# Expert matrices loaded with two neighbouring rows per partition, and features kept in pairs

## The chip, the cores and the metric

The kernel runs on one core of a Trainium2 chip. The metric is the device time of one execution in microseconds (us), lower is better. All times below come from runs of the kernel before the change and from one profiled execution of it.

## The reference

Two layers of a transformer over 256 latent tokens and 256 context tokens of 1,024 features each. A layer has two parts. The first modulates its input, projects it once, and feeds four mixers (three attentions and a 2-D Fourier transform), gates and merges them and projects the result. The second is the one that the change touches, a mixture of 16 experts in which each expert chooses 32 tokens of a stream:

```python
def expert_choice_ffn(h, w_router, w_gate, w_up, w_down):
    cap = max(1, EC_CAPACITY * n // N_EXPERTS)            # 32
    aff = softmax(einsum("bnd,de->bne", h, w_router))
    sel_w, sel_idx = lax.top_k(swapaxes(aff, 1, 2), cap)
    xs = vmap(lambda hb, ib: hb[ib])(h, sel_idx)
    a = einsum("becd,edf->becf", xs, w_gate)
    u = einsum("becd,edf->becf", xs, w_up)
    y = einsum("becf,efd->becd", silu(a) * u, w_down) * sel_w[..., None]
    # rows of y are added back at their tokens
```

Both parts end in a residual and a layer norm. In layer 0 both streams go through the mixture (64 rows an expert), in layer 1 the latents alone (32 rows). All data are float32. An expert has three matrices of 1,024 x 1,024, 4 MB each, so the two mixtures read 2 x 16 x 12 MB.

## The kernel before, in words

**Loads.** Weights stream from HBM in tiles of 1 MB, nearly all issued by SyncE (SP) in one fixed order. `ex_raw` (L359) describes a quarter of an expert matrix, 256 rows: `(k p) n -> p k n` with p = 128, so partition p receives row p and row 128 + p, two runs of 4 KB that lie 512 KB apart in HBM and side by side in SBUF. Where the tile is one piece (`raw`, `w8`, `q8`, `k8`, `cst`, `wbr`) one DMA brings it (L376). Where it is a list (`p`, `pt`, `b4`: two tiles of 512 KB; `wbs`: four of 256 KB) each piece has a DMA of its own (L374). The last expert's `w_down` comes by columns instead, a quarter of the columns of all rows at a time, in runs of 1 KB (L365). The planner at the end of the program (L1682 to L1720) keeps the loads up to 16 tiles ahead of their use, in the order in which the units of work use them; a tile's load waits until the work that last used its buffer is done. `ring` says which buffers the experts take in turn: in layer 1 a cycle of 18 holds one `p` and one `pt`, in layer 0 no list.

**An expert.** `gu0` and `gu1` multiply the gathered token rows by gate and up, taking the quarters in the order in which they are loaded (gate 0, up 0, gate 1, and so on); `swiglu` is on ScalarE (ACT, L1077) and VectorE (DVE, L1078, L1079); `down0` and `down1` transpose the result in four blocks of 128 features on TensorE (PE: L1102 in layer 0, L1129 in layer 1), copy it out of PSUM on ACT, and multiply by `w_down` (L1109, L1136). Tokens are gathered by one-hot products (`gather`, L996, transposes at L1012; `gather_one`, L1023, transposes at L1038), and a group of four experts is scattered back by `scat` (L1146). The last group and the last expert have their own steps (`scat_hl` L1152, `scat_start` L1195, `last_hT`, `last_down` L1216, `last_scat`).

**Feature order.** Contraction block kt holds the features kt x 128 to kt x 128 + 127 everywhere. Transposes take contiguous blocks of 128 columns: `turned` (L904) for the router, the gathers and the downs. `mod_tr` (L243, products at L250) and `load_b`, `load_ln` (L171, L178) bring modulation vectors, biases and norm gains into the same order, `small_loads` (L453) the router's weights, and `g_bcast` (L315) spreads a gate vector over all partitions and copies it out of PSUM on ACT (L324).

**Order of work.** SP and GpSimd (POOL) issue in the program's order. PE, ACT and DVE are ordered by the framework's scheduler, except where `inorder` fixes it. In layer 0, `load_b` and `load_ln` for layer 1 run within the gates (L1383).

Of the kernel before, what the change touches and what calls it, by code (L numbers as in the profile page):

```python
# [16 lines left out]
D = 1024  # L17
# [69 lines left out]
def trunk(ctx: ExitStack, tc: tile.TileContext, x, c, ctx_in, c_ctx, w_mod, b_mod, w_in, qk_gain,  # L87
# [52 lines left out]
    def load_consts(l):  # L140
        """The mixers' tables, which give their place to weights once a layer's attention is done."""
        mix_cst.append(big([128, N_MIX], "cst"))
        nc.sync.dma_start(mix_cst[-1], consts[:, 0:N_MIX])
        if l == 0:
            nc.sync.dma_start(route_cst, consts[:, N_MIX:N_CONST])
# [10 lines left out]
    def ones():  # L156
        # the last column of the triangle
        return const("tri")[:, 127:128].to_broadcast([128, 128])
# [12 lines left out]
    def load_b(l):  # L171
        bsrc = t2([48, 128])
        G.dma_start(bsrc, b_mod[l].rearrange("(k p) -> k p", p=128))
        p = ps_t([128, 48])
        T.transpose(p, bsrc, ident[0:48, 0:48])
        V.tensor_copy(bT[l], p)

    def load_ln(l):  # L178
        lsrc = t2([32, 128])
        for n, v in enumerate((ln1_g, ln1_b, ln2_g, ln2_b)):  # L180
            G.dma_start(lsrc[8 * n:8 * n + 8], v[l].rearrange("(k p) -> k p", p=128))
        p = ps_t([128, 32])
        T.transpose(p, lsrc, ident[0:32, 0:32])
        V.tensor_copy(lnT[l].rearrange("p n k -> p (n k)"), p)
# [25 lines left out]
    def mod_mm(l, ch, group):  # L210
        """Partial products of one chunk, in rows 2q and 2q + 1 of each quadrant (q the chunk's place in its four)."""
# [14 lines left out]
    def mod_acc(l, ch, group):  # L226
        """As mod_mm, but the chunks of a group add up in a bank of their own."""
# [15 lines left out]
    def mod_tr(l, group):  # L243
        """Sums of up to four chunks, feature-major."""
# [4 lines left out]
        for g in range(4):  # L249
            T.matmul(p[:, g], mrows[l, group][:, g * 128:g * 128 + 128], sel[:, 0:8], start=True, stop=True)  # L250
# [8 lines left out]
    def mod_first(kp):  # L259
        """Shift and scale of two feature tiles, the first layer's."""  # L260
# [32 lines left out]
    def affine(l, half):  # L293
        """u = z * A + B, feature-major: the modulation, with the norm's own gain and bias folded in."""
# [20 lines left out]
    def g_bcast(l, m, j, ns=range(2)):  # L315
        t = gbc[l, m, j] if (l, m, j) in gbc else b4([128, D])
        gbc[l, m, j] = t
        for n in ns:
# [5 lines left out]
            A.activation(t[:, n * 512:n * 512 + 512], p, AF.Copy)  # L324

# [33 lines left out]
    def ex_raw(l, e, kind, q):  # L359
        w = {"g": w_gate, "u": w_up, "d": w_down}[kind]  # L360

        if e == NE - 1 and kind == "d":
            # the last expert's share of the output comes by columns
# [4 lines left out]
        rows = w[l, e, q * 256:q * 256 + 256, :].rearrange("(k p) n -> p k n", p=128)  # L368

        def go(t):  # L370
# [4 lines left out]
            else:  # L375
                nc.sync.dma_start(t, rows)  # L376
        return (("ex", l, e, kind, q), [128, 2, D], go)

    def ex_w(l, e, kind, k, c, n):
        """Rows k * 128.. and columns c..c + n of an expert's matrix."""  # L380
# [24 lines left out]
    def inorder(*engines):  # L405
        """What the block puts on these engines issues after the previous such block's work."""
# [10 lines left out]
    def split(key, src, alloc, eng=V):  # L417
        """hi + lo parts, each exact in the product's 12-bit significand."""
# [25 lines left out]
    def small_loads(l):  # L444
# [8 lines left out]
        G.dma_start(wr[:, 0:8], w_router[l].rearrange("(k p) e -> p k e", p=128))  # L453
        st_["small"] = {"gq": gq, "snk": snk, "wr": wr}

    def layer(l):
# [7 lines left out]
        def ut_alloc():  # L464
            if last:
                # a tile per stream: the context's go after the projections
# [33 lines left out]
        def bias_table():  # L500
            """Per-row relative-position bias, 8x, flipped into token order."""
# [47 lines left out]
        def rope(src, t, nh):  # L549
            """Rotates src [128, nh, 64] in place."""  # L550
# [11 lines left out]
        def post_norm(m, t):  # L562
            """Values aside; the norm's factors."""
# [15 lines left out]
        def post_vec(m, t):  # L579
            """norm and rotation of one token tile, split."""  # L580
# [26 lines left out]
        def post_tr(m, t):  # L607
            """q blocks [hi | lo] ([lo | hi] for the second kv head), k blocks [hi | hi] x 2, [lo0 | lo1]."""
# [19 lines left out]
        def br_out(m, src, kv, ts):  # L628
            """src [128, kv, tokens] to the branch, split."""
# [195 lines left out]
        def residual(dst, z, key):  # L825
            """alpha times the norm's output, from its normalised rows."""
# [6 lines left out]
        def y0_mm(kt):  # L833
            """Left half of the output: one merged feature tile's share, all tokens."""
# [45 lines left out]
        NS = NT // 2  # L880

        def route_weights():
            """The norm and the modulation folded into the router: logits = rstd * (h.wA - mean * sum(wA)) + B.w"""
# [15 lines left out]
        def turned(t, hf):  # L899
            """Half of the features of a token tile, feature-major."""  # L900
            pt = ps_t([128, 4, 128])
            u = t2([128, 4, 128])
            for k in range(4):
                T.transpose(pt[:, k], st_["h"][t][:, (4 * hf + k) * 128:(4 * hf + k) * 128 + 128], ident)  # L904
# [3 lines left out]
        def route_half(t, hf):  # L908
            """Router products of one half of the features of a token tile."""
# [4 lines left out]
            for k in range(4):  # L914
                # rows 0..15 of a quadrant sum its share; rows 16..31 are not used
# [20 lines left out]
        def route(t):  # L936
            """Router probabilities of one token tile; its rows normalised."""
# [14 lines left out]
        def rows(t):  # L952
            """Normalises a token tile."""
# [795 lines left out]
```

## Time and profile before

| | us |
|---|---|
| median of three runs | 1805.77 |
| lowest and highest | 1802.51, 1806.38 |
| span of the profiled execution, first to last instruction | 1799.7 |

The profiled execution is known by its span; what lies around the span is seen only as the difference to the median, 6.1 us. The two mixtures lie at about 540 to 1010 us (layer 0) and 1320 to 1790 us (layer 1) of that span. The page divides the span into 40 slices of 45 us; DMA there is the mean busy share of the core's 16 DMA engines. A busy PE in such a slice may still be a PE that waits often and briefly, because the ends of pipelined matmuls are modelled. The idle time before an instruction, and what ended it, is in the views by waits and in order of time.

### The profile page before, as it was taken

To read this page: it belongs to the slowest core of one execution; us is meant where nothing else is said; L and a number is where in the kernel's file an instruction comes from. 1 tells how busy PE (TensorE), PEld (TensorE's weight loads), DVE (VectorE), ACT (ScalarE), POOL (GpSimd) and SP (SyncE) were. 2 spreads that over 40 slices of the span, in tenths; PEclk is the share of its full clock that TensorE was granted. 3 is DMA by queue.
4 is the path that set the end of the run, shared out by engine and by line. 5 is a ranking of instruction groups with operands and counts; after the bars stand their busy time and mean duration, and the time that the engine had idled before them with its cause. 6 is when DMAs were issued, how large, how long until landed. Compare 5 with 4: busy or idle time off the path is not lost.

```text
span 1799.7 us, 22915 instructions
## 1 busy us (share of the span) xinstructions
PE 1575.4 (88%) x9291; PEld 892.1 (50%) x9291; DVE 694.8 (39%) x1378; ACT 432.3 (24%) x929; POOL 129.7 (7%) x176
## 2 busy tenths in 40 slices
PE   7999999999989989899998899999978666667666
PEld 4767777768864333323332578888832211112112
DVE  3454453554452332222222585747543111102114
ACT  2343433343231110201200354544321001001000
POOL 1200112111110000000000320111100000000000
PEclk9999999999989999999999999999989889888888
DMA  9444344444559999999999664646889999999996
GB/s 310 164 149 157 119 167 107 164 140 165 216 208 365 374 408 409 409 409 409 409 409 403 234 240 169 216 111 236 327 317 409 409 409 409 409 409 409 409 409 245
DMA packets 194120, 533.04 MB, mean 296 GB/s; under 512 B 9520, under 2 KB 61088, under 8 KB 194016
## 3 DMA queue, kind: packets, MB, share of 16 engines
q1 hardware_dynamic: 192016, 527.49, 76.9%
q0 software_dynamic: 1856, 4.02, 1.3%
q8 instruction: 73, 1.20, 0.3%
q14 instruction: 31, 0.25, 0.0%
q10 hardware_dynamic: 144, 0.07, 0.0%
HBM read 530.50 MB, written 1.05 MB: 295 GB/s over the span
## 4 chain that ended last, share of the span: by engine, by line
PE 67%; DMA 15%; issue 10%; DVE 5%; ACT 2%; POOL 1%; SPq 0%; ACTq 0%; DVEq 0%; POOLq 0%
PE mm L771 14%; PE mm L1088 12%; PE mm L531 7%; DMA w<-in_w_up_dram 6%; PE mm L1109 5%; DMA raw<-in_w_up_dram 4%; PE mm L782 3%; PE pt L217 2%; PE mm L1122 2%; PE mm L851 2%; PE ps L1005 2%; DMA w<-in_w_down_dram 2%; PE ps L643 2%; PE pt L724 1%; PE ps L642 1%
## 5 line engine op out<-in xcount | busy, mean ns | idle before, releaser
L771 PE MATMUL mm<-w,b 128*128 128x512 f32 (+1 forms) x1536 | 292.6, 342 | 0.3 <-DVE b L424 0.3
L771 PEld LDWEIGHTS mm<-w,b 128*128 128x128 f32 x1536 | 236.8, 189 | 47.7 <-issue 18.6
L1077 ACT ACTIVATE t<-mm 128x512 f32<-128x512 f32 (+1 forms) x32 | 19.0, 594 | 663.2 <-PE mm L1122 352.1
L1078 DVE SCALAR_TENSOR_TENSOR t<-t,mm 128x512 f32<-128x512 f32 (+1 forms) x32 | 21.9, 684 | 358.6 <-ACT t L1077 358.5
L424 DVE TENSOR_TENSOR b<-raw,b 128x1024 fp32r<-128x1024 f32 (+1 forms) x95 | 112.7, 1189 | 122.7 <-ACT b L422 119.7
L531 PE MATMUL mm<-b,w 128*128 128x512 f32 (+1 forms) x720 | 148.9, 360 | 5.2 <-ACT b L422 3.6
L531 PEld LDWEIGHTS mm<-b,w 128*128 128x128 f32 x720 | 115.9, 192 | 30.7 <-ACT b L422 4.0
L422 ACT ACTIVATE b<-raw 128x1024 fp32r<-128x1024 f32 (+1 forms) x96 | 97.9, 1021 | 128.9 <-PE mm L771 97.5
L1095 DVE TENSOR_TENSOR k<-mm,b 32x512 f32<-32x512 f32 (+1 forms) x96 | 53.1, 553 | 187.5 <-PE mm L1109 84.6
L1088 PE MATMUL mm<-w,b 128*64 128x512 f32 x480 | 116.9, 596 | 2.1 <-DMA w<-in_w_gate_dram 1.2
L1122 PE MATMUL mm<-w,b 128*32 128x512 f32 x416 | 82.5, 665 | 26.9 <-DMA w<-in_w_up_dram 22.3
L800 POOL TENSOR_TENSOR b<-b,t 128x256 f32<-128x256 f32 x72 | 56.4, 798 | 521.6 <-DVE t L794 502.4
L1122 PE MATMUL mm<-raw,b 128*32 128x512 f32 x256 | 55.4, 733 | 30.8 <-DMA raw<-in_w_up_dram 16.1
L782 PE MATMUL mm<-w,wbs 128*128 128x512 f32 (+1 forms) x384 | 78.4, 339 | 0.1
L1088 PEld LDWEIGHTS mm<-w,b 128*64 128x64 f32 x480 | 37.9, 137 | 70.3 <-issue 63.9
L1088 PE MATMUL mm<-raw,b 128*64 128x512 f32 x280 | 70.9, 594 | 0.7 <-DMA raw<-in_w_gate_dram 0.7
L782 PEld LDWEIGHTS mm<-w,wbs 128*128 128x128 f32 x384 | 61.2, 188 | 8.8 <-ACT w L631 0.3
L1109 PE MATMUL mm<-w,t 128*64 128x512 f32 x240 | 58.4, 612 | 2.9 <-ACT t L1104 2.9
L1122 PEld LDWEIGHTS mm<-w,b 128*32 128x32 f32 x416 | 16.3, 116 | 86.8 <-DMA w<-in_w_up_dram 41.4
L681 ACT ACTIVATE p<-ps,st 128x512 f32<-128x512 f32 (+1 forms) x72 | 43.6, 613 | 55.3 <-DVE st L679 55.3
L1146 PE MATMUL ps<-k,wbs 128*128 128x512 f32 x72 | 39.7, 671 | 4.7 <-DVE k L1095 3.7
L1122 PEld LDWEIGHTS mm<-raw,b 128*32 128x32 f32 x256 | 9.8, 118 | 65.8 <-DMA raw<-in_w_up_dram 28.7
(373 smaller groups left out, 2232.6 us busy)
## 6 DMA issues: line engine op xcount, KB each, us to landing
w<-in_w_up_dram SPq DMA_DIRECT2D x64, 1024.0 KB, 18.1
w<-in_w_down_dram SPq DMA_DIRECT2D x59, 1024.0 KB, 16.6
raw<-in_w_mod_dram SPq DMA_DIRECT2D x48, 1024.0 KB, 5.2
w<-in_w_gate_dram SPq DMA_DIRECT2D x48, 1024.0 KB, 18.3
raw<-in_w_in_dram SPq DMA_DIRECT2D x46, 1024.0 KB, 6.3
raw<-in_w_down_dram SPq DMA_DIRECT2D x35, 1024.0 KB, 16.1
raw<-in_w_up_dram SPq DMA_DIRECT2D x34, 1024.0 KB, 15.3
raw<-in_w_gate_dram SPq DMA_DIRECT2D x33, 1024.0 KB, 15.3
```

Source lines behind the costliest of these rows:

```text
L422: A.activation(hi, src, AF.Copy)
L424: eng.tensor_tensor(lo, src, hi.bitcast(F32), op=OP.subtract)
L531: T.matmul(p, uu(kt, t * 128, t * 128 + 128), ww[:, kt % 2, a:n], start=kt == 0 and i == 0, stop=kt == 7 and i == 2)
L681: A.activation(P[:, hh, a:b], s[:, hh, a:b], AF.Exp, scale=0.125, bias=nm[:, n:n + 1], accum_out=rs[:, n:n + 1])
L771: T.matmul(p, ww[:, kt], uu(kt, 0, NTOK), start=n == 0, stop=n == 23)
L782: T.matmul(p, ww[:, k, o:o + 128], br[i][:, j, k], start=n == 0, stop=n == 5)
L800: G.tensor_tensor(m, m, e[:, c], op=OP.add)
L1088: T.matmul(p[fh * 64:fh * 64 + 64], xs[kt // 4][:, kt % 4, e % 4], ex_w(l, e, kind, kt, fh * 512, 512), start=kt == 0, stop=kt == 7)
L1095: V.tensor_tensor(dst, pd[q], g, op=OP.mult)
L1109: T.matmul(pd[dh * 64:dh * 64 + 64], hT[:, q, fh * 64:fh * 64 + 64], ex_w(l, e, "d", f, dh * 512, 512), start=f == 0, stop=f == 7)
L1122: T.matmul(p[r:r + 32], xs[kt // 4][:, kt % 4, e % 4], ex_w(l, e, kind, kt, fh * 512, 512), start=kt == 0, stop=kt == 7)
L1146: T.matmul(p[:, dh], loc["sm", gr][:, s, t], loc["y", gr][s][:, dh * 512:dh * 512 + 512], start=True, stop=True)
```

## The change

A quarter of an expert matrix is now loaded as `(p k) n -> p k n`: partition p receives rows 2p and 2p + 1, which are neighbours in HBM, as one run of 8 KB. Block kt of a contraction therefore holds every second feature of a stretch of 256: `paired(kt)` gives the columns 256 (kt // 2) + kt % 2, in steps of 2. All that meets these blocks is put in the same order: the transposes of `turned`, `gather`, `gather_one`, `down0` and `down1` read with a step of two elements; so do the products in `mod_tr` for all chunks but the first four; `load_b` and `load_ln` transpose both the plain and the paired order; the router's weights are loaded in pairs; `g_bcast` puts the plain order back with a copy that writes with a step of two. The matmuls with expert weights read the same places of the tiles as before. Loads into lists keep their pieces of 4 KB a partition, and the last expert's `w_down` keeps its columns and the plain order. Comments were taken out as well, which is left out here.

```diff
     def load_b(l):
-        bsrc = t2([48, 128])
-        G.dma_start(bsrc, b_mod[l].rearrange("(k p) -> k p", p=128))
-        p = ps_t([128, 48])
-        T.transpose(p, bsrc, ident[0:48, 0:48])
-        V.tensor_copy(bT[l], p)
+        bsrc = t2([24, 256])
+        G.dma_start(bsrc, b_mod[l].rearrange("(k p) -> k p", p=256))
+        p = turned_both(bsrc, 24)
+        b = bT[l].rearrange("p (q k) -> p k q", k=2)
+        V.tensor_copy(b[:, :, 0:8], p[:, 0, :, 0:8])
+        V.tensor_copy(b[:, :, 8:24], p[:, 1, :, 8:24])
 
     def load_ln(l):
-        lsrc = t2([32, 128])
+        lsrc = t2([16, 256])
         for n, v in enumerate((ln1_g, ln1_b, ln2_g, ln2_b)):
-            G.dma_start(lsrc[8 * n:8 * n + 8], v[l].rearrange("(k p) -> k p", p=128))
-        p = ps_t([128, 32])
-        T.transpose(p, lsrc, ident[0:32, 0:32])
-        V.tensor_copy(lnT[l].rearrange("p n k -> p (n k)"), p)
+            G.dma_start(lsrc[4 * n:4 * n + 4], v[l].rearrange("(k p) -> k p", p=256))
+        p = turned_both(lsrc, 16)
+        b = lnT[l].rearrange("p n (q k) -> p k (n q)", k=2)
+        V.tensor_copy(b[:, :, 0:8], p[:, 1, :, 0:8])
+        V.tensor_copy(b[:, :, 8:16], p[:, 0, :, 8:16])
...
+    def paired(kt):
+        c = kt // 2 * 256 + kt % 2
+        return slice(c, c + 255, 2)
+
+    def turned_both(src, n):
+        p = ps_t([128, 2, 2, n])
+        for k in range(2):
+            T.transpose(p[:, 0, k], src[:, k * 128:k * 128 + 128], ident[0:n, 0:n])
+            T.transpose(p[:, 1, k], src[:, k:k + 255:2], ident[0:n, 0:n])
+        return p
@@ mod_tr
         for g in range(4):
-            T.matmul(p[:, g], mrows[l, group][:, g * 128:g * 128 + 128], sel[:, 0:8], start=True, stop=True)
+            c = paired(g) if group[0] > 3 else slice(g * 128, g * 128 + 128)
+            T.matmul(p[:, g], mrows[l, group][:, c], sel[:, 0:8], start=True, stop=True)
@@ g_bcast
-            A.activation(t[:, n * 512:n * 512 + 512], p, AF.Copy)
+            A.activation(t[:, n * 512:n * 512 + 512].rearrange("p (q i k) -> p q k i", q=2, k=2),
+                         p.rearrange("p (q k i) -> p q k i", q=2, k=2), AF.Copy)
@@ ex_raw
-        rows = w[l, e, q * 256:q * 256 + 256, :].rearrange("(k p) n -> p k n", p=128)
+        rows = w[l, e, q * 256:q * 256 + 256, :].rearrange("(p k) n -> p k n", p=128)
...
-                nc.sync.dma_start(t, rows)
+                nc.sync.dma_start(t.rearrange("p k n -> p (k n)"), rows.rearrange("p k n -> p (k n)"))
@@ small_loads
-        G.dma_start(wr[:, 0:8], w_router[l].rearrange("(k p) e -> p k e", p=128))
+        G.dma_start(wr[:, 0:8].rearrange("p (q k) e -> p q (k e)", k=2),
+                    w_router[l].rearrange("(q p k) e -> p q (k e)", p=128, k=2))
@@ turned
-                T.transpose(pt[:, k], st_["h"][t][:, (4 * hf + k) * 128:(4 * hf + k) * 128 + 128], ident)
+                T.transpose(pt[:, k], st_["h"][t][:, paired(4 * hf + k)], ident)
@@ gather
-                T.transpose(p[:, q].rearrange("p n e c -> p (n e c)"), rows[:, q * 128:q * 128 + 128], ident)
+                T.transpose(p[:, q].rearrange("p n e c -> p (n e c)"), rows[:, paired(q)], ident)
@@ gather_one
-                T.transpose(p[:, k].rearrange("p q c -> p (q c)"), rows[:, k * 128:k * 128 + 128], ident)
+                T.transpose(p[:, k].rearrange("p q c -> p (q c)"), rows[:, paired(k)], ident)
@@ down0
-                T.transpose(p[:, q], a[:, q * 128:q * 128 + 128], ident)
+                T.transpose(p[:, q], a[:, paired(q)], ident)
@@ down1
-                T.transpose(p[:, q], a[:, q * 128:q * 128 + 128], ident[0:64, 0:64])
+                T.transpose(p[:, q], a[:, paired(q)], ident[0:64, 0:64])
```

## Rows read from the trace of the kernel before

**Rows 1.** The page of the profiled execution, part 2: the span in 40 slices of 45 us, busy tenths of PE and of the 16 DMA engines, and GB/s.

```profile
...
PE   7999999999989989899998899999978666667666
...
DMA  9444344444559999999999664646889999999996
GB/s 310 164 149 157 119 167 107 164 140 165 216 208 365 374 408 409 409 409 409 409 409 403 234 240 169 216 111 236 327 317 409 409 409 409 409 409 409 409 409 245
...
```

**Rows 2.** Busy time by stretch, from one call that cuts the span into eight: stretch, its length, busy us of each engine with its instructions, granted TensorE clock, busy share of the 16 DMA engines, GB/s.

```profile
...
540.00:650.00 110.00, 101.28 (x496) 43.11 (x494) 35.10 (x73) 19.09 (x54) 1.47 (x4) 1.00 0.96 377
650.00:945.00 295.00, 276.58 (x1258) 97.34 (x1256) 75.84 (x131) 30.83 (x67) 1.47 (x4) 0.99 1.03 409
945.00:970.00 25.00, 19.45 (x85) 5.20 (x81) 2.04 (x3) 1.20 (x2) 0.00 (x0) 1.00 1.03 409
970.00:1010.00 40.00, 38.52 (x186) 17.29 (x187) 16.30 (x29) 7.30 (x14) 3.07 (x5) 1.00 0.96 344
...
1340.00:1768.00 428.00, 297.79 (x2150) 91.13 (x2150) 76.02 (x154) 30.92 (x78) 3.57 (x6) 0.87 1.03 409
...
```

**Rows 3.** DMA packets of the stretch 700 to 900 us, in layer 0's mixture, where the data packets are 4 KB (the 1,245 small ones are completion marks): count, bytes, rate.

```profile
...
DMA packets 21195, 81.81 MB, mean 409 GB/s; under 512 B 1245, under 2 KB 1245, under 8 KB 21186
...
```

**Rows 4.** The same for 989 to 993 us, the last expert's column loads, whose runs are 1 KB.

```profile
...
DMA packets 1381, 1.39 MB, mean 348 GB/s; under 512 B 21, under 2 KB 1381, under 8 KB 1381
...
```

**Rows 5.** The same for 1031.3 to 1032.486 us, the second load of the constants (L143), whose runs are 7,936 bytes.

```profile
...
DMA packets 64, 0.51 MB, mean 428 GB/s; under 512 B 0, under 2 KB 0, under 8 KB 64
...
```

**Rows 6.** PE's weight loads in order of time, 940 to 972 us: start, busy us, line, operation, tiles, count, and in brackets the idle time before the first of them and what ended it.

```profile
...
943.87 0.14 PEld L1088 LDWEIGHTS mm<-w,b 128*64 128x64 f32 x2 [0.28 <-issue]
...
946.87 0.20 PEld L1088 LDWEIGHTS mm<-w,b 128*64 128x64 f32 x4 [1.13 <-DMA w<-in_w_up_dram]
...
949.42 0.20 PEld L1088 LDWEIGHTS mm<-w,b 128*64 128x64 f32 x4 [1.50 <-DMA w<-in_w_gate_dram]
...
951.99 0.20 PEld L1088 LDWEIGHTS mm<-w,b 128*64 128x64 f32 x4 [1.51 <-DMA w<-in_w_up_dram]
...
954.55 0.20 PEld L1088 LDWEIGHTS mm<-w,b 128*64 128x64 f32 x4 [1.50 <-DMA w<-in_w_gate_dram]
...
957.11 0.20 PEld L1088 LDWEIGHTS mm<-cst,b 128*64 128x64 f32 x4 [1.50 <-DMA cst<-in_w_up_dram]
...
964.79 0.20 PEld L1109 LDWEIGHTS mm<-wbr,t 128*64 128x64 f32 x4 [0.83 <-DMA wbr<-in_w_down_dram]
...
967.35 0.20 PEld L1109 LDWEIGHTS mm<-raw,t 128*64 128x64 f32 x4 [1.50 <-DMA raw<-in_w_down_dram]
...
969.96 0.19 PEld L1088 LDWEIGHTS mm<-raw,b 128*64 128x64 f32 x2 [1.56 <-PE mm L1109]
...
```

**Rows 7.** The chain that ended last within 940 to 1010 us, in order of time: start, us, what.

```profile
...
951.25 18.61 DMA raw<-in_w_gate_dram
...
969.99 1.04 PE mm L1088 x2
...
996.08 0.70 DVE t L1079
...
```

**Rows 8.** Expert loads by rows (L376) that were issued from 640 to 660 us: time from issue to landing.

```profile
...
DMA to landing us min/median/max: 6.9/9.6/11.3
```

**Rows 9.** The same, issued from 740 to 760 us.

```profile
...
DMA to landing us min/median/max: 18.1/18.5/18.8
```

**Rows 10.** DMA issues by tile and source: count, KB each, median us from issue to landing.

```profile
...
p<-in_w_gate_dram SPq DMA_DIRECT2D x16, 512.0 KB, 16.5
pt<-in_w_up_dram SPq DMA_DIRECT2D x16, 512.0 KB, 15.3
...
p<-in_w_down_dram SPq DMA_DIRECT2D x8, 512.0 KB, 15.9
pt<-in_w_down_dram SPq DMA_DIRECT2D x8, 512.0 KB, 15.5
...
```

**Rows 11.** What PE waited for from 1340 to 1760 us, longest in total first: us in total, times, longest.

```profile
...
PE mm L1122 <- DMA w<-in_w_up_dram: 22.3, 18, 1.5
PE mm L1122 <- DMA raw<-in_w_up_dram: 16.1, 12, 1.6
...
```

**Rows 12.** PE's matmuls in order of time at the end of layer 1 (columns as in rows 6).

```profile
...
1783.97 1.07 PE L1223 MATMUL mm<-w,t 128*32 128x256 f32 x16 [1.17 <-DMA w<-in_w_down_dram]
...
```

**Rows 13.** Weight loads of PE by line and shape: line, engine, operation, tiles, shape, count | busy us, mean ns of one | idle us before them.

```profile
...
L1012 PEld LDWEIGHTS pt<-idsel,t 128*128 128x128 f32 x84 | 8.8, 142 | 39.8 <-DVE t L1008 33.8 <-ACT t L1009 4.1 <-issue 1.6
...
L1102 PEld LDWEIGHTS pt<-idsel,t 128*128 128x128 f32 x60 | 7.2, 146 | 12.4 <-DVE t L1079 10.3 <-ACT wbs L1070 1.8 <-issue 0.2
...
L250 PEld LDWEIGHTS pt<-idsel,t 128*128 128x128 f32 x48 | 5.8, 191 | 0.8 <-issue 0.3 <-ACT b L422 0.2
...
L904 PEld LDWEIGHTS pt<-idsel,pt 128*128 128x128 f32 x16 | 2.0, 159 | 1.6 <-PE pt L928 1.1 <-issue 0.4
...
```

**Rows 14.** PE in order of time, 76 to 88 us, around the transpose in `load_ln` (columns as in rows 6).

```profile
...
82.97 0.24 PE L183 MATMUL pt<-idsel,t 32*128 32x32 f32 x1
83.14 5.11 PE L771 MATMUL mm<-w,b 128*128 128x512 f32 x21
```

**Rows 15.** PE in order of time, the first 8 us (columns as in rows 6).

```profile
...
7.42 1.08 PE L274 MATMUL ps<-raw,c_st 128*32 128x256 f32 x8 [0.89 <-DMA raw<-in_w_mod_dram]
```

**Rows 16.** ACT by line and shape (columns as in rows 13): the copy in `g_bcast`.

```profile
...
L324 ACT ACTIVATE b<-mm 128x512 f32<-128x512 f32 x12 | 7.2, 599 | 7.9 <-PE mm L321 7.9
...
```

## The prediction

> **What bounds the kernel now.** I read the page's slices first: PE is near full nearly everywhere, and the DMA engines are full in two stretches, at 409 GB/s, slices 15 to 22 and 31 to 39 [rows 1]. These are the two mixtures. Where two resources look full, the one that ends last must be found stretch by stretch, so I cut the span at the places where the picture changes [rows 2].
>
> In layer 1 from 1340 to 1768 us the DMA share is 1.03 throughout and PE is busy for 298 of 428 us: the loads bind. The waits say the same, with PE's longest ones on tiles of `w_up` that were still landing [rows 11], and a wait for `w_down` as late as 1784 us [rows 12].
>
> Layer 0 is less plain. From 650 to 945 us DMA is full, but PE is busy for 277 of 295 us. Here PE sets the pace and the loads run ahead. Only from 945 to 970 us does PE fall to 19.5 of 25. The reader is to see in PE's weight loads how the usual idle time of 0.28 us between pairs becomes 0.8 to 1.6 us at the head of each tile: eight such waits, 11.03 us together, less eight times 0.28 us is 8.8 us lost to late tiles; the one named after PE is a wait for a tile of `w_gate` in the chain [rows 6, 7]. From 970 us on the chain is PE alone until 996 us, and PE is busy for 38.5 of the 40 us to 1010 us [rows 2, 7]. So layer 0 can give no more than about 9 us to a faster load.
>
> **What a longer run is worth.** The rate depends on the length of the run. At 4 KB the trace shows 409 GB/s, which is 16 x 4,096 B / 409 = 160.2 ns a packet on each of 16 engines; at 1 KB 348 GB/s, or 47.1 ns; at 7,936 B 64 packets in 1.186 us, four on each engine, or 296.5 ns, 428 GB/s [rows 3, 4, 5]. The third row also shows that a run above 4 KB isn't cut up. A run of 8,192 B isn't in the trace. The line through the rows of 1 and 4 KB gives 311 ns, the one through 4 KB and 7,936 B gives 305.6 ns. Two packets of 4 KB cost 320.4 ns. A tile is eight runs of 8 KB on each engine, so it gains 0.075 to 0.118 us of its 2.563 us (1,048,576 B at 409 GB/s). I take 0.11 us, near the upper end, because 7,936 B is nearly the length in question; the rest is left for the completion marks, which that row hardly holds.
>
> The Trainium skill speaks against that ("DMA: Bandwidth & Descriptors", Specifications): it puts line rate at runs of 512 B and more, by which the change would bring nothing; the trace disagrees, with 348, 409 and 428 GB/s [rows 3 to 5]. The same page of the Trainium skill (Why small descriptors are slow) gives a fixed cost of about 3 cycles a packet, which at its 850 MHz is an estimate of 0.028 us a tile, and by it the sum below would be about 1800 us.
>
> **Layer 1.** 428 us at 2.563 us is 167 tiles. One is left out for a norm's gain and bias (two loads of 512 KB on SP, by the code). Lists keep their runs of 4 KB: the issues of `p` and `pt`, 24 each at half a tile [rows 10], are 24 tiles, of which the code's ring puts two ahead of 1340 us, so 22. That leaves 144 tiles x 0.11 = **15.8 us** (10.8 to 17.0). PE doesn't stand in the way, with 30% of the stretch idle; the last loads, by columns, keep their 1 KB, and what follows them is only shifted. DMA stays last.
>
> **Layer 0.** A faster queue gains only while it is never empty. Loads issued from 640 to 660 us land after 9.6 us, those from 740 to 760 us after 18.5 us [rows 8, 9]: around 650 us the queue is short, because tiles wait for buffers that PE still reads, and then it grows. I count the gain from there: to 957 us, 307 / 2.563 = 120 tiles x 0.11 = 13.2 us (9.0 to 14.2). This is more than the 8.8 us that PE lost, so I take **8.8 us**. Next late is PE itself, in its unbroken run after 970 us. The four microseconds left over end as tiles that lie ready earlier.
>
> **What is added.** `load_b` and `load_ln` run twice each and have three more transposes a time, 12 in all. In `load_ln` one holds PE for 0.17 us, from 82.97 to the next product at 83.14 us [rows 14]. Three run in the first 8 us, where PE waits 0.9 us for weights anyhow [rows 15]; nine x 0.17 = **1.5 us** on the path. Their second copy on DVE, four in all, is hidden by DVE's slack beside PE in the gates; uncovered it would be under 1 us.
>
> Transposes and products with a step of two read their stationary operand with that step: 60 loads at L1102, 56 of the 84 at L1012 in layer 0, 48 at L904 and 12 at L1038 (the code's counts), 176 at about 0.14 us; and 40 of the 48 at L250 at 0.19 us [rows 13]. Layer 1's at L1012 and L1129 lie under the wait for tiles. No row shows a stepped weight load. From below: nothing, as no engine reads fewer elements. From above: twice as long, 176 x 0.14 + 40 x 0.19 = 32.2 us, all on PE's path. I take nothing, as the number of elements, rows and instructions is the same. In the Trainium skill ("SBUF — State Buffer", Door 1) two reads in a 16-byte line suffice for full rate, which a step of two float32 gives; no run here shows it.
>
> `g_bcast` writes with a step on ACT, 12 copies at 0.6 us [rows 16]: between nothing and another 7.2 us if each took twice as long and none were hidden; I take nothing, since the element count stays. No DMA is added and none changes its place on SP or POOL; those of biases, gains and router weights have fewer, longer runs. The planner's order stays, and no wait is added.
>
> **Sum.** -15.8 - 8.8 + 1.5 = -23.1 us on a span of 1799.7 us, so 1776.6 us. The median run is 6.1 us above the span; the forecast is 1805.8 - 23.1 = 1782.7 us, **1783 us**. A change under 0.2%, 3.6 us, could not be told from none.
>
> **Rivals.**
> 1. Layer 0 gives nothing: tiles stay as late as the buffers that PE frees, or PE's order comes out worse. For it speaks that PE has only 18 of 295 us free there [rows 2]; against it the queue that grows to 18.5 us [rows 9]. 1805.8 - 15.8 + 1.5 = 1791.5 us.
> 2. The rate stays at 409 GB/s, because full-size tiles from many rows are limited by something else than the price of a packet, or because the run is cut in two. For it: the row of 7,936 B is a stretch of 1.2 us only. Against it: that row, and the line of the other two. Only the added 1.5 us are left, 1807.3 us. This is also what the line rate that the Trainium skill states would come to.
> 3. Slower: stepped weight loads. If each took twice as long, PE would pay 32.2 us in the router, the modulation and layer 0's mixture, where PE is the pace already, and the gain would be outrun: 1782.7 + 32.2 = 1814.9 us. It decides from a price of about 72% more a load (23.1 / 32.2). Nothing in the profile speaks for it, and nothing excludes it.
>
> **How the numbers follow.** Forecast 0.66, rival 1 0.15, rival 2 0.11, rival 3 0.08. The forecast's own spread, from 0.118 us a tile with the transposes hidden (-17.0 - 8.8 = -25.8) to 0.075 us (-10.8 - 8.8 + 1.5 = -18.1), is 1780 to 1788 us; one run differs from another by some 4 us. The range from 1777 to 1800 us holds it and rival 1, about 0.8. Faster 0.81, same 0.11 (rival 2), slower 0.08 (rival 3).
>
> **What would show it.** Right: packets of 8 KB in the mixtures and a rate near 428 GB/s from 650 to 960 and in layer 1; PE's waits at the head of tiles gone between 945 and 970 us; each of layer 1's experts about 1.2 us shorter. Weight loads at L1102 and L1012 still near 0.14 us. Wrong: a rate of 409 or less; stepped loads of 0.24 us and more; an order of PE's work in which a down waits for something that it did not wait for before.

## The result

| | median us | lowest, highest | kernel before beside it | ratio, 95% interval |
|---|---|---|---|---|
| changed kernel | 1794.53 | 1793.57, 1796.26 | 1805.42 | 0.9944 [0.9932, 0.9957] |
| again, second series | 1796.11 | 1794.31, 1798.30 | 1804.69 | 0.9953 [0.9940, 0.9965] |
| again, third series | 1796.20 | 1794.11, 1799.29 | 1805.19 | 0.9950 [0.9936, 0.9963] |

The change makes the kernel faster by 8.6 to 10.9 us by the medians, some 0.5%. The forecast was 1783 us, a gain of 22.8 us against the median of the three runs known then. The time lies in the range, but less than half of the gain came.

The profiled execution took 1795.16 us with a span of 1793.4, so 1.8 us lie around the span. The 6.1 us that I put there for the kernel before were mostly, by some 4 us, the distance of its profiled execution from the median. The difference between the kernels doesn't hang on that, but the two spans alone, 6.3 us apart, show less than the medians do.

### The profile page after: what moved, and what is told of

Read it like the earlier page. It is cut to its first block, busy times and chain, and to the rows that moved or that the text cites. A ratio compares the mean times of both kernels' runs of the same rounds, so it can differ in the third digit from the quotient of the medians.

```text
span 1793.4 us, 22944 instructions
## 1 busy us (share of the span) xinstructions
PE 1582.9 (88%) x9303; PEld 906.0 (51%) x9303; DVE 695.3 (39%) x1382; ACT 432.4 (24%) x929; POOL 129.4 (7%) x176
## 4 chain that ended last, share of the span: by engine, by line
PE 68%; DMA 14%; issue 10%; DVE 5%; ACT 2%; POOL 1%; SPq 0%; ACTq 0%; DVEq 0%; POOLq 0%
PE mm L792 14%; PE mm L1109 12%; PE mm L552 7%; PE mm L1130 6%; DMA w<-in_w_up_dram 4%; PE mm L803 3%; DMA raw<-in_w_up_dram 2%; PE pt L235 2%; PE mm L872 2%; DMA w<-in_w_down_dram 2%; PE ps L1026 2%; PE ps L1167 2%; PE ps L664 2%; PE pt L745 1%; PE ps L663 1%
## 5 line engine op out<-in xcount | busy, mean ns | idle before, releaser
L1116 DVE TENSOR_TENSOR k<-mm,b 32x512 f32<-32x512 f32 (+1 forms) x96 | 53.1, 553 | 189.8 <-PE mm L1157 84.5
L1109 PEld LDWEIGHTS mm<-raw,b 128*64 128x64 f32 x280 | 22.1, 137 | 39.8 <-issue 37.7
```

The lines of the kernel that those rows point to most:

```text
L1109: T.matmul(p[fh * 64:fh * 64 + 64], xs[kt // 4][:, kt % 4, e % 4], ex_w(l, e, kind, kt, fh * 512, 512), start=kt == 0, stop=kt == 7)
L1116: V.tensor_tensor(dst, pd[q], g, op=OP.mult)
```

## The profile after

First the 40 slices, as in [rows 1], and the stretches, as in [rows 2].

```profile
...
PE   7999999999989999999999899999978766767765
...
DMA  9544344535568999999999566546879999999996
GB/s 306 170 142 164 118 165 113 165 119 187 183 239 317 371 406 422 421 422 421 420 421 411 180 243 211 186 115 217 315 317 402 419 419 420 419 420 419 420 420 245
...
```

```profile
...
650.00:945.00 295.00, 275.91 (x1248) 99.90 (x1250) 73.47 (x130) 32.84 (x73) 1.47 (x4) 0.99 1.01 419
945.00:970.00 25.00, 23.52 (x111) 8.03 (x108) 4.36 (x6) 1.19 (x2) 0.00 (x0) 1.00 1.01 421
970.00:1010.00 40.00, 37.81 (x184) 16.65 (x181) 16.75 (x28) 6.61 (x13) 2.81 (x4) 1.00 0.82 293
...
1340.00:1768.00 428.00, 307.96 (x2228) 99.56 (x2220) 77.17 (x157) 31.97 (x80) 3.58 (x6) 0.88 1.01 416
...
```

Both mixtures load at about 420 GB/s where they loaded at 409. PE's busy time in 945 to 970 us rose from 19.45 to 23.52 us: the waits for tiles at the end of layer 0 are gone. What did not come is the rate of 428 GB/s. The packets from 700 to 900 us, as in [rows 3]:

```profile
...
DMA packets 11562, 84.24 MB, mean 421 GB/s; under 512 B 1285, under 2 KB 1285, under 8 KB 1285
...
```

Every data packet is now 8 KB long, none is cut. At 421 GB/s one takes 16 x 8,192 / 421 = 311.3 ns, which is the value that the line through [rows 3, 4] had given, 311.

PE's weight loads from 954 to 970 us, as in [rows 6]:

```profile
...
956.73 0.14 PEld L1109 LDWEIGHTS mm<-w,b 128*64 128x64 f32 x2 [0.29 <-issue]
957.15 0.14 PEld L1109 LDWEIGHTS mm<-w,b 128*64 128x64 f32 x2 [0.28 <-issue]
...
961.54 0.56 PEld L1123 LDWEIGHTS pt<-idsel,t 128*128 128x128 f32 x4 [1.67 <-DVE t L1100]
962.98 0.20 PEld L1130 LDWEIGHTS mm<-raw,t 128*64 128x64 f32 x4 [0.88 <-ACT t L1125]
963.46 0.14 PEld L1130 LDWEIGHTS mm<-raw,t 128*64 128x64 f32 x2 [0.28 <-issue]
...
969.47 0.14 PEld L1109 LDWEIGHTS mm<-raw,b 128*64 128x64 f32 x1 [0.29 <-issue]
969.90 0.14 PEld L1109 LDWEIGHTS mm<-raw,b 128*64 128x64 f32 x1 [0.29 <-issue]
...
```

No idle time here is ended by a DMA any more; 0.28 us is the usual pace of a pair. The reader is to see what these waits were worth: PE comes to the first weight load of the next expert at 969.47 us, against 969.96 before [rows 6]. The gain of that stretch went almost wholly into making up what PE had fallen behind by 930 us. The starts of the same two instructions of ACT show it, first in the kernel before and then in the changed one:

```profile
...
930.63 0.60 ACT L1077 ACTIVATE t<-mm 128x512 f32<-128x512 f32 x1 [19.26 <-PE mm L1088]
...
970.17 0.63 ACT L1157 ACTIVATE t<-k 128x512 fp32r<-128x512 f32 x1 [9.04 <-DVE k L1097]
...
```

```profile
...
936.10 0.60 ACT L1098 ACTIVATE t<-mm 128x512 f32<-128x512 f32 x1 [19.26 <-PE mm L1109]
...
970.95 0.63 ACT L1178 ACTIVATE t<-k 128x512 fp32r<-128x512 f32 x1 [8.02 <-DVE k L1118]
...
```

So the changed kernel is 5.5 us behind at the first and 0.8 us at the second. Where the 5.5 us come from this pair of traces doesn't show: the profiled execution of the kernel before was itself some 4 us faster than its median.

The stepped reads are a part of it. They are in the weight loads and products by line and shape (columns as in [rows 13]), the changed kernel's first:

```profile
...
L1033 PEld LDWEIGHTS pt<-idsel,t 128*128 128x128 f32 x84 | 13.3, 207 | 38.8 <-DVE t L1029 34.3 <-ACT t L1030 2.9 <-issue 1.6
L1123 PEld LDWEIGHTS pt<-idsel,t 128*128 128x128 f32 x60 | 9.2, 210 | 12.3 <-DVE t L1100 10.3 <-ACT wbs L1091 1.8
L269 PEld LDWEIGHTS pt<-idsel,t 128*128 128x128 f32 x48 | 6.1, 195 | 0.8 <-issue 0.3 <-ACT b L442 0.2
...
L1033 PE MATMUL pt<-idsel,t 128*128 128x128 f32 x84 | 20.1, 324 | 18.1 <-DVE t L1029 17.0 <-ACT t L1030 1.1
L1123 PE MATMUL pt<-idsel,t 128*128 128x128 f32 x60 | 11.5, 306 | 6.1 <-DVE t L1100 4.7 <-ACT wbs L1091 1.4
L1150 PE MATMUL pt<-idsel,t 64*128 64x64 f32 x60 | 10.4, 300 | 23.8 <-DVE t L1100 23.4 <-ACT wbs L1091 0.5
...
```

The same products in the kernel before:

```profile
...
L1012 PE MATMUL pt<-idsel,t 128*128 128x128 f32 x84 | 18.2, 301 | 18.3 <-DVE t L1008 16.8 <-ACT t L1009 1.2
L1102 PE MATMUL pt<-idsel,t 128*128 128x128 f32 x60 | 10.6, 290 | 6.1 <-DVE t L1079 4.7 <-ACT wbs L1070 1.4
L1129 PE MATMUL pt<-idsel,t 64*128 64x64 f32 x60 | 6.8, 233 | 23.8 <-DVE t L1079 23.4 <-ACT wbs L1070 0.5
...
```

A transpose's weight load rose from 142 to 207 ns and from 146 to 210 [rows 13]; the products in `mod_tr` (L269), whose plain load took 191 ns already, went to 195 only (8 of these 48 are still read plainly). The loads overlap PE's products, so what PE itself shows is less: 16 to 23 ns a transpose of 128 rows, and 67 ns for the downs of 64 rows, which lie in layer 1, where PE has idle time.

The step did something else too, in `gather_one`, which gathers the first experts of a mixture. There DVE copies the first 128 columns of a block of 256 out of PSUM and ACT the other 128 after it. A transpose of neighbours needs one of these copies; a transpose of every second column needs both. These transposes in the kernel before, in the changed kernel, and in the version below that takes the step in the copies:

```profile
...
L1038 PE MATMUL mm<-idsel,t 128*128 128x128 f32 x12 | 3.8, 362 | 2.2 <-DVE t L1032 2.0
...
```

```profile
...
L1059 PE MATMUL mm<-idsel,t 128*128 128x128 f32 x12 | 3.5, 380 | 3.6 <-ACT t L1054 3.6
...
```

```profile
...
L1066 PE MATMUL mm<-idsel,t 128*128 128x128 f32 x12 | 4.0, 367 | 2.1 <-DVE t L1060 2.0
...
```

PE's idle time before them rose from 2.2 to 3.6 us, and what ends it is now ACT's copy.

## The experiments

The theory: a packet has a fixed price of about 9 ns beside its bytes, so 8 KB is worth 0.075 us a tile and not 0.11; the waits in layer 0 were worth less than 8.8 us; and the stepped weight loads cost several microseconds on PE's path. Rivals: the steps are free and PE's lag has another source; layer 0 gives nothing; what 8 KB gave is not a matter of packets.

**The steps undone, the loads kept.**

```diff
     def paired(kt):
-        c = kt // 2 * 256 + kt % 2
-        return slice(c, c + 255, 2)
+        return slice(kt * 128, kt * 128 + 128)
...
-            T.transpose(p[:, 1, k], src[:, k:k + 255:2], ident[0:n, 0:n])
+            T.transpose(p[:, 1, k], src[:, k * 128:k * 128 + 128], ident[0:n, 0:n])
```

> The changed kernel with its 8 KB loads, but every transpose and product reads its features one beside the other again (the second transpose of the biases and gains stays). Features so meet the rows of other features: the numbers are not the reference's, the amount of work is. Theory T (the stepped reads lengthen TensorE's weight loads from 140 to about 209 ns on the engine's own path, and this is most of the 10 us by which the changed kernel falls behind outside the two stretches where its loads gain): weight loads of the turned hidden tiles back at 140 ns, 6 to 9 us under the changed kernel, so 1785.5 to 1788.5. Rival A (the steps cost nothing, the lag comes from the extra transposes and from the loads' collisions): 1794.5, as the changed kernel. Rival B (half and half): 1790 to 1792.

Measured: 1791.63 us (before 1804.10), ratio 0.9924 [0.9907, 0.9941]. Against the changed kernel's three ratios that is 0.0020 to 0.0029 less, 3.6 to 5.2 us, uncertain by about 4: less than theory T said, near rival B, and by itself hardly apart from nothing. This edit gives `gather_one` its shorter wait back as well. The weight loads are back where they were:

```profile
...
L1032 PEld LDWEIGHTS pt<-idsel,t 128*128 128x128 f32 x84 | 8.8, 141 | 40.8 <-DVE t L1028 34.8 <-ACT t L1029 4.1 <-issue 1.6
...
L1122 PEld LDWEIGHTS pt<-idsel,t 128*128 128x128 f32 x60 | 7.2, 146 | 12.4 <-DVE t L1099 10.3 <-ACT wbs L1090 1.8 <-issue 0.2
...
```

PE's lag at 930 us is nearly as large without the steps as with them. The instruction of ACT that starts at 930.63 us in the kernel before starts here at

```profile
...
934.63 0.60 ACT L1097 ACTIVATE t<-mm 128x512 f32<-128x512 f32 x1 [19.26 <-PE mm L1108]
...
```

that is 4.0 us behind, where the changed kernel was 5.5 us behind, and 5.0 and 4.6 in its other two profiles. So the steps don't explain most of that lag.

**The steps alone, with the loads of before.**

```diff
-        rows = w[l, e, q * 256:q * 256 + 256, :].rearrange("(p k) n -> p k n", p=128)
+        rows = w[l, e, q * 256:q * 256 + 256, :].rearrange("(k p) n -> p k n", p=128)
...
-                nc.sync.dma_start(t.rearrange("p k n -> p (k n)"), rows.rearrange("p k n -> p (k n)"))
+                nc.sync.dma_start(t, rows)
```

> The changed kernel with the loads of the kernel before (two runs of 4 KB per partition): the order of the features alone, with the steps and the extra transposes. Features meet the rows of other features, so the numbers are not the reference's; the work is that of the changed kernel. Theory T: the kernel before plus about 10 us, 1813 to 1817, and a DMA rate of 409 GB/s at 1400 to 1700 us, lists apart. Rival A (steps free): 1805 to 1807. The difference to the changed kernel is then what the 8 KB runs give in both layers: about 16 us by T (5.6 in layer 0 and 10.8 in layer 1), 22 to 25 by my forecast of 0.11 us a tile.

Measured: 1807.73 us (before 1804.10), ratio 1.0023 [1.0011, 1.0034], so the new order of the features, its extra transposes and its longer wait in `gather_one` included, costs 4.2 us (2.0 to 6.1). It is a real cost, and again less than half of the 10 us that theory T had added up from one pair of traces. That sum was wrong in its method: by the starts of the same ACT instructions, kernels whose work up to 500 us is the same stand there from 0.66 to 2.94 us behind the kernel before, so a lag of a few microseconds in one pair of traces is partly chance.

**The 8 KB loads in layer 0 alone, and in layer 1 alone.** The lines that matter (in the second kernel `l == 1`):

```diff
-        rows = w[l, e, q * 256:q * 256 + 256, :].rearrange("(p k) n -> p k n", p=128)
+        near = l == 0
+        rows = w[l, e, q * 256:q * 256 + 256, :].rearrange("(p k) n -> p k n" if near else "(k p) n -> p k n", p=128)
...
-            else:
+            elif near:
                 nc.sync.dma_start(t.rearrange("p k n -> p (k n)"), rows.rearrange("p k n -> p (k n)"))
+            else:
+                nc.sync.dma_start(t, rows)
```

> The changed kernel with the 8 KB loads in layer 0 alone (layer 1 loads two runs of 4 KB, and there features meet the rows of other features, so the numbers are not the reference's). Against the same kernel with no 8 KB loads at all (1807.7 us): my forecast's term is -8.8, 1798.9; the waits counted by TensorE's product starts at 945 to 970 us give -5 to -6, 1802 to 1803; the rival that layer 0 gives nothing at the end, 1807.7.

> The changed kernel with the 8 KB loads in layer 1 alone (layer 0 loads two runs of 4 KB, and there features meet the rows of other features). Against the same kernel with no 8 KB loads (1807.7 us): my forecast's term is 144 x 0.11 = -15.8, 1791.9; by the rate of the trace, 144 x 0.075 = -10.8, 1797; if a part of the stretch is not bound by loads, as the lags in the traces suggest, -9, 1798.7.

> The changed kernel itself, beside the kernels that have one half of its loads each. If the two layers add up, its gain over the kernel with no 8 KB loads (1807.7 us) is the sum of the gains of the two halves: -14 to -16 by the trace, 1792 to 1794.

Measured, with 1804.69 us for the kernel before: layer 0 alone 1804.97, ratio 1.0004 [0.9995, 1.0013]; layer 1 alone 1798.39, ratio 0.9965 [0.9953, 0.9976]; both 1796.11, ratio 0.9953. With the steps alone at 1.0023, from the series before, four differences follow; each is uncertain by about 3 us (the intervals' half-widths, 0.0009 to 0.0013, added in squares).

| what 8 KB runs give | without the other layer's | beside the other layer's | forecast |
|---|---|---|---|
| in layer 0 | 1.0004 - 1.0023: -3.4 us | 0.9953 - 0.9965: -2.2 us | -8.8 us |
| in layer 1 | 0.9965 - 1.0023: -10.5 us | 0.9953 - 1.0004: -9.2 us | -15.8 us |

The layers add up, within the uncertainty. Layer 1's gain is that of the measured rate: 144 tiles x (1,048,576 B / 409 - 1,048,576 B / 421 GB/s = 0.073 us) = 10.5 us. Layer 0's is small: of its two values only the first is clear of nothing. The stretch from 945 to 970 us in the kernel with the steps alone, and in the one with 8 KB in layer 0:

```profile
...
945.00:970.00 25.00, 20.68 (x92) 6.10 (x90) 3.94 (x6) 1.19 (x2) 0.00 (x0) 1.00 1.03 409
...
```

```profile
...
945.00:970.00 25.00, 23.52 (x112) 7.99 (x109) 4.36 (x6) 1.19 (x2) 0.00 (x0) 1.00 1.01 421
...
```

The steps alone already raise PE's busy time from 19.45 to 20.68 us here, and in the kernel with 8 KB in layer 1 alone, which loads layer 0 in the same way and came there later still (7.3 us behind at 930 us, against 3.0), it is 22.28 us: a PE that comes later waits less. So the two parts of the change are not independent in these traces, the waits pay for some of a lag and then can't be gained a second time. The table's two values for a layer, 1.2 to 1.3 us apart, don't resolve it.

**Runs of 2 KB**, from the kernel before:

```diff
-                nc.sync.dma_start(t, rows)
+                for c in range(0, D, 512):
+                    nc.sync.dma_start(t[:, :, c:c + 512], rows[:, :, c:c + 512])
```

> The kernel before with each expert tile that goes to one buffer loaded in two halves of its columns, so in runs of 2 KB, twice the packets and two issues a tile; the result is the same. Theory P (each packet has a fixed price beside its bytes, which the step from 4 KB at 409 GB/s to 8 KB at 421 puts at 9 ns of a DMA engine): 2 KB packets take some 84.5 ns, a tile 2.70 us, the rate at 700 to 900 us is 388 GB/s, layer 1 loses 144 x 0.14 = 20 us, layer 0 its cover and then 120 x 0.14 = 17 us, so 1838 to 1846. Rival (what 8 KB gave is not a matter of packets, but of the descriptors' or the rows' order): 405 to 409 GB/s and 1803 to 1810. Rival 3 cycles a packet: 0.028 us a tile doubled, 400 to 403 GB/s and 1812 to 1818.

Measured, one run: 1849.59 us. The packets from 700 to 900 us:

```profile
...
DMA packets 40047, 77.30 MB, mean 387 GB/s; under 512 B 2354, under 2 KB 2354, under 8 KB 40039
...
```

A packet of 2 KB takes 16 x 2,048 / 387 = 84.7 ns, where theory P said 84.5. Now four lengths lie on one line: 47.1, 84.7, 160.2 and 311.3 ns at 1, 2, 4 and 8 KB are 0.0369 ns a byte and 9.2 ns a packet, each within 0.2 ns. That settles the price, and the rival that 8 KB was not a matter of packets, which expected 405 GB/s or more here, falls. The Trainium skill ("DMA: Bandwidth & Descriptors", Why small descriptors are slow) has about 3 cycles, an estimate of 3.5 ns at the page's 850 MHz; the runs show more than twice that. The time came out above the expected 1838 to 1846 us, because layer 0 lost more than I had given it: by the starts of the same ACT instructions in both traces, it falls behind from about 800 us on and is 24.5 us behind at 970 us, where I had expected 17. Layer 1 adds 21.8 us from 1382 to 1780 us.

**A step of four in place of two.**

```diff
-        c = kt // 2 * 256 + kt % 2
-        return slice(c, c + 255, 2)
+        c = kt // 4 * 512 + kt % 4
+        return slice(c, c + 509, 4)
```

> The changed kernel with a step of 4 in blocks of 512 features in place of 2 in blocks of 256 wherever a whole block is there (the small gather of the first experts stays at 2). Features meet the rows of other features, so the numbers are not the reference's. One look at the duration of the weight loads of the transposes. If a stepped read has one price: 209 ns as at step 2, and a time of 1794 to 1796. If the price grows with the 16-byte pieces that are touched: those double once more, to 340 to 400 ns each, and the time is 1806 to 1816. If it is a float32 load's plain length at step 1 that was hidden: 192 ns.

Measured, one run: 1812.98 us. The weight loads:

```profile
...
L1033 PEld LDWEIGHTS pt<-idsel,t 128*128 128x128 f32 x84 | 12.0, 209 | 47.0 <-ACT t L1030 47.0
L269 PEld LDWEIGHTS pt<-idsel,t 128*128 128x128 f32 x48 | 10.7, 304 | 0.8 <-issue 0.3 <-ACT b L442 0.2
L1123 PEld LDWEIGHTS pt<-idsel,t 128*128 128x128 f32 x60 | 8.9, 210 | 12.3 <-DVE t L1100 10.3 <-ACT wbs L1091 1.8
...
```

For a transpose the step has one price, 207 to 210 ns at two as at four, as the first of the three expectations had it. The time that went with this expectation (1794 to 1796) is missed by 17 us. The products of `mod_tr` show a part of it: means of 191, 195 and 304 ns at steps of one, two and four (the 8 plain ones included), 48 x 0.109 = 5.2 us. Most of the rest is a wait. DVE copies the first 256 columns that a gather transposes and ACT the other 256; a step of four spans both, so that by the code the first transpose needs both copies, as in `gather_one` above:

```profile
...
L1033 PE MATMUL pt<-idsel,t 128*128 128x128 f32 x84 | 16.4, 321 | 27.8 <-ACT t L1030 27.8
...
```

PE's idle time before these transposes is 27.8 us, ended by ACT each time, where the changed kernel's is 18.1 us: 9.7 us more. The two together make some 15 of the 17 us, an estimate from one run.

**The step taken by the copies.** In the gathers and ahead of the down products the result passes through ACT and DVE on its way out of PSUM anyway. This version lets those read with a step, and PE's transposes read neighbours.

```diff
+            rv = rows.rearrange("p (q k i) -> p q k i", q=2, k=2)
+            gv = pg.rearrange("p (q i k) -> p q k i", q=2, k=2)
...
-            A.activation(rows[:, 256:512], pg[:, 256:512], AF.Copy)
+            A.activation(rv[:, 1], gv[:, 1], AF.Copy)
...
-                T.transpose(p[:, q].rearrange("p n e c -> p (n e c)"), rows[:, paired(q)], ident)
+                T.transpose(p[:, q].rearrange("p n e c -> p (n e c)"), rows[:, q * 128:q * 128 + 128], ident)
...
+            if e < NE - 1:
+                pg, pu = (p.rearrange("p (i k) -> p k i", k=2) for p in (pg, pu))
+                av = a.rearrange("p (k i) -> p k i", k=2)
+            A.activation(av, pg, AF.Tanh, scale=0.5)
...
-                T.transpose(p[:, q], a[:, paired(q)], ident)
+                T.transpose(p[:, q], a[:, halves(q)], ident)
```

> The changed kernel with the same result, but in the gathers and ahead of the down products the step is taken by the copies and the activation that read PSUM anyway, so that TensorE's transposes there read one feature beside the other; the router's transposes and the modulation's products stay stepped. Theory T: weight loads of these transposes back at about 140 ns, the copies and the activation longer by 30 ns or so (as the gates' copy went from 597 to 627), mostly beside TensorE's work: 3 to 5 us under the changed kernel, 1789.5 to 1791.5. Rival A (steps on TensorE cost nothing): 1794.5. Rival C (stepped reads of PSUM by the activation and by VectorE cost as much again, and stand on the path from the products to the down products): 1794 to 1799.

> The version with the steps in the copies once more, beside the changed kernel on the same chip. If the steps on TensorE that it spares (gathers and down products, 23 ns more of each transpose in the products' rows, and the stretch of 1328 to 1382 us, where it lost 0.1 us and the changed kernel 2.9) cost what the traces say, it is 2 to 3 us under the changed kernel; if its first result was chance, the two are within 1 us.

> The changed kernel beside the version with the steps in the copies: 8.5 to 10.5 us under the kernel before, as in its first two series.

Measured: 1793.19 us, ratio 0.9936 [0.9921, 0.9951], and in the second series 1793.18, ratio 0.9934 [0.9920, 0.9948], where the changed kernel beside it took 1796.20. Beside the changed kernel, in the second series, it takes 3.0 us less, as theory T said, though each of its two intervals overlaps those of the changed kernel; its runs went from 1791.6 to 1795.4, the changed kernel's from 1794.1 to 1799.3. The transposes' weight loads are back at 144 and 148 ns, and `gather_one` is back at its shorter wait (2.1 us, above), so this run doesn't part the two. Its instructions on ACT and DVE, in the second series:

```profile
...
L1110 DVE SCALAR_TENSOR_TENSOR t<-t,mm 128x512 f32<-128x512 f32 x16 | 11.0, 688 | 128.5 <-ACT t L1109 128.5
...
L1109 ACT ACTIVATE t<-mm 128x512 f32<-128x512 f32 x16 | 9.6, 597 | 308.1 <-PE mm L1120 308.1
...
L1035 DVE COPY t<-ps 128x256 f32<-128x256 f32 x21 | 8.9, 423 | 18.5 <-PE ps L1030 18.4
...
```

The changed kernel's contiguous ones:

```profile
...
L1099 DVE SCALAR_TENSOR_TENSOR t<-t,mm 128x512 f32<-128x512 f32 x16 | 11.0, 688 | 128.5 <-ACT t L1098 128.5
...
L1098 ACT ACTIVATE t<-mm 128x512 f32<-128x512 f32 x16 | 9.6, 597 | 307.5 <-PE mm L1109 307.5
...
L1029 DVE COPY t<-ps 128x256 f32<-128x256 f32 x21 | 8.9, 424 | 16.0 <-PE ps L1026 15.9
...
```

Not one is longer, so rival C falls, and the 30 ns that I had allowed were not needed either.

Part of what this version saves is at the start of layer 1's mixture, where each kernel comes from a wait of 5.8 us of PE for DVE. From the end of this wait to the first product of the next expert it takes 4.62 us, as the kernel before does, and the changed kernel 4.84, with the longer wait in `gather_one`. What follows isn't the steps'. The stretches 1330 to 1335 and 1335 to 1340 us of the changed kernel and then of the kernel with the steps alone (columns as in [rows 2]), which has the same instructions there and came out of its wait 0.7 us later, at 1327.61 us:

```profile
...
1330.00:1335.00 5.00, 3.99 (x18) 1.11 (x22) 1.21 (x5) 1.47 (x5) 0.00 (x0) 0.50 0.00 0
1335.00:1340.00 5.00, 5.00 (x40) 1.31 (x36) 0.00 (x0) 0.00 (x0) 0.00 (x0) 0.78 0.69 254
...
```

```profile
...
1330.00:1335.00 5.00, 3.88 (x26) 1.03 (x22) 1.26 (x5) 1.46 (x5) 0.00 (x0) 0.53 0.01 3
1335.00:1340.00 5.00, 5.00 (x53) 1.32 (x44) 0.00 (x0) 0.00 (x0) 0.00 (x0) 1.00 0.64 228
...
```

The granted clock stays at its lower level, 0.50 (1.2 GHz), for all of the first stretch in the changed kernel and is back at 1.00 (2.4 GHz) only within the second; with the steps alone it is back before the second begins. From the end of the wait to the products of the tile `b` the changed kernel takes 11.0 us in all its three profiles, the kernel with the steps alone 9.4, the kernel before 9.3 and this version 9.4 and 10.1. With the same stepped reads the clock came back late and early, so this difference isn't a price of the steps, and a part of the 3.0 us may be the clock's.

## Why the prediction was wrong

**The mechanism of the gain was right; its two terms were mis-sized, and the steps were put at nothing.** The steps add 4.2 us; the loads give 2.2 to 3.4 us in layer 0 and 9.2 to 10.5 in layer 1. With either layer taken first that is -8.5 us, against -23.1 in my sum. That it meets the measured ratio of 0.9953 is no test, since the differences are taken along a chain that ends there; what they show is the split.

**A tile's gain, 0.11 us: 0.073 us.** This step was out by 5.3 to 6.6 us in layer 1. I had the right value, the line through [rows 3, 4], and put it at the low end because [rows 5] held nearly the length in question. But that row was 0.5 MB out of the middle of one load, four packets on each engine in 1.186 us, while [rows 3] was a stream of 200 us. What is nearest to a mixture's load is a full queue, not a similar length. Why the short row looked faster than the line (296.5 against 302 ns) stays open, but for its lack of completion marks, of which the stream of 8 KB has one for every eight packets (1,285 for 10,277).

**The waits in layer 0, 8.8 us: 2.2 to 3.4 us.** That all of them went is as forecast; their size was out by 5.4 to 6.6 us, as much as layer 1's term. It was read from PE's weight loads, as idle time beyond the usual 0.28 us. After a wait these rows show four loads at once, where the usual rows show two: a part of that idle time is made up right behind it. In the products' rows the idle time that a tile ended is 4.0 us in all:

```profile
...
L1088 PE MATMUL mm<-w,b 128*64 128x512 f32 x32 | 7.7, 605 | 2.1 <-DMA w<-in_w_gate_dram 1.2 <-DMA w<-in_w_up_dram 0.9
L1109 PE MATMUL mm<-raw,t 128*64 128x512 f32 x24 | 5.6, 600 | 1.3 <-ACT t L1104 0.7 <-DMA raw<-in_w_down_dram 0.6
L1088 PE MATMUL mm<-cst,b 128*64 128x512 f32 x8 | 1.9, 605 | 0.6 <-DMA cst<-in_w_up_dram 0.6
...
L1088 PE MATMUL mm<-raw,b 128*64 128x512 f32 x1 | 0.6, 614 | 0.7 <-DMA raw<-in_w_gate_dram 0.7
...
```

That is the kernel before, 945 to 970 us: 1.2 + 0.9 + 0.6 + 0.6 + 0.7. Modelled ends may hide some of it; the traces put the same ACT instruction 4.7 us closer to the kernel before at 970 than at 930 us in the changed kernel, 0.7 in the kernel with the steps alone and 2.1 in the one with 8 KB in layer 1 alone, so 2.6 to 4.0 for the loads.

**The stepped reads, nothing: with the extra transposes 4.2 us (2.0 to 6.1).** I took the lower end, because the number of elements stayed. The rule that I set beside it, of the Trainium skill ("SBUF — State Buffer", Door 1), that two reads in a 16-byte line suffice, is not borne out by the transposes' 142 to 207 ns; in the products of `mod_tr`, with 191 to 195, it nearly is. Rival 3, the slower case, had the right place and the wrong size: 176 loads at 65 ns more would be 11.4 us, if PE's own path took all of it, and of the 65 ns PE's products show 16 to 23. And the sentence that no wait is added was wrong: the step made `gather_one`'s transposes wait for ACT's copy, 1.4 us. Worked out from the rows, as an estimate, layer 0's downs and gathers cost 60 x 16 + 56 x 23 ns = 2.2 us and this wait 1.4 us, together most of the 4.2. No run separates the two: steps undone and the step in the copies take away both.

**The extra transposes, 1.5 us: not resolved.** The kernel with the steps undone keeps them and is 12.5 us faster than the kernel before, where the loads' two gains make 12.6 to 12.7; the uncertainty of some 3 us leaves room for 1.5 as for nothing. `g_bcast` went from 0.599 to 0.631 us a copy, 12 x 0.032 = 0.4 us, near the nothing that I took.

**Rival 1** (layer 0 gives nothing, 1791.5 us) came out nearest in time, but by luck, for other reasons: its rate of 0.11 us a tile was too high, and layer 0 gives something, of which the steps take back a part or all. In the changed kernel's own trace layer 0 indeed ends where it ended before. **Rival 2** is excluded, the rate did rise.

## What to carry to other kernels

Fit a packet's price from two saturated streams in the same trace, and trust that line over a short lone transfer that happens to have the right length. When a new data layout reorders a contraction, put the step into a copy out of PSUM that ACT or DVE makes anyway rather than into PE's transposes, and look whether a stepped read spans what two engines write: it then waits for the later of them. Where PE both waits for loads and is then made slower, count the gain and the cost together: the waits can absorb a part of the cost, and can be gained only once.

## What the runs showed of the hardware

The rate of a full DMA queue still grows beyond 4 KB runs: 348, 387, 409 and 421 GB/s at 1, 2, 4 and 8 KB. The line through them has its limit at 16 / 0.0369 ns = 434 GB/s, which is worked out from the four and not reached in any run. The Trainium skill ("DMA: Bandwidth & Descriptors", Specifications) puts a fabric ceiling at 435 GB/s; the line agrees.

A float32 transpose on PE loads its stationary operand in 142 ns from neighbouring columns and in 207 to 210 from every second or fourth. The other products that were stepped, those of `mod_tr`, go from 191 to 195 and 304 ns at the same steps. Reads of every second column of PSUM by ACT (597 ns at 512 columns) and DVE (688 ns) took no longer than contiguous ones.
